# Where the weight splits stand around the last sums of a seven-product group, in a two-layer encoder trunk

## The chip, the core and the metric

The kernel runs on one core of one Trainium2 chip. The metric is the device time of one execution in microseconds; three runs of the kernel before gave 930.63, 929.8 and 930.38, so its median is 930.38 us.

The engines that matter here are TensorE (PE in the profile, with its weight loads as PEld), VectorE (DVE), ScalarE (ACT), GpSimd (POOL), which here mostly issues transfers that add to their destination, and SyncE (SP), which issues the plain transfers. Each engine works through its own instructions strictly in the order in which they were written into the program; an instruction waits until the data and the buffers that it needs are there, and everything behind it on the same engine waits with it.

## What is computed

The input is one sequence of 256 tokens of width 1024 in float32. There are two layers, each with a half-weighted SwiGLU channel mixer, a mixing part with two kinds of attention, and a second channel mixer; a norm closes the trunk. The channel mixers do most of the work:

```python
D_MODEL = 1024
SEQ = 256
DEPTH = 2
D_FF = 2816

def swiglu(h, w_gate, w_up, w_down):
    return (jax.nn.silu(h @ w_gate) * (h @ w_up)) @ w_down

    for l in range(DEPTH):
        x = x + 0.5 * swiglu(rms_norm(x, ffn1_norm[l]), ffn1_w_gate[l], ffn1_w_up[l], ffn1_w_down[l])
        ...
        x = x + jnp.concatenate([out_a, out_b], axis=-1) @ w_out[l]

        x = x + 0.5 * swiglu(rms_norm(x, ffn2_norm[l]), ffn2_w_gate[l], ffn2_w_up[l], ffn2_w_down[l])
    return rms_norm(x, final_norm)
```

## The kernel before

**Precision and the split.** Every float32 matrix is held as a sum of two parts in the type that TensorE multiplies fast: a high part, which is the value rounded by a cast on ACT, and a low part, which is the value less the high part, subtracted on DVE. A product is then three matmuls (high by high, low by high, high by low). So each weight tile that TensorE multiplies by must first be cast by ACT and subtracted by DVE. This pair of instructions is called a *split* here. The weights come in *steps* of 128 rows x 4 x 512 columns (1 MB), and each step is split in two halves, a and b, by `emit_split` (L191): `act.copy(h_, r_)` and `dve.tensor_tensor(l_, r_, f(h_), op=ALU.subtract)`.

**Groups.** A channel mixer goes through the 2816 hidden columns in five groups of 512 and a last one of 256. A group computes gate and up for 256 tokens, then the hidden block (silu of gate, times up). The hidden block is turned by TensorE (`turn`, L681: transposes, then a cast on ACT and a subtraction on DVE for each of two banks), so that it can be multiplied by the down weights, one group later: while group g works on its gate and up products, the down products of group g - 1 are woven in.

**Groups by seven products.** For some groups gate and up are not computed by eight products of a quarter of the work each (two token halves x two halves of the width x gate and up) but by seven, after the manner of Strassen and Winograd (`by_seven`, L632). The sums of tokens that this takes are made once in a channel mixer. The sums of weights are made in each group: two by transfers of POOL that add the incoming weights onto a tile in place (`gather`, L126), two by DVE (`plus`, L131; two instructions each, `prep` of a step). What the products give is put together by DVE additions (`put`, L637). `SEVEN` (L31) says which groups are done so: groups 2, 3 and 4 in the first channel mixer of the first layer, and groups 1, 2, 3 and 4 in the other three. These three are called *runs of four* here.

A group by seven products uses nine steps of weights, one after the other. Groups 2 to 4 use them in the order p1, p7, p2, p3, down 0, p5, p6, p4, down 1; the first group of a run (the branch `else` of `by_seven`) in the order p1, p2, down 0, p3, p7, p5, p6, p4, down 1. Each product is 12 matmuls of 128x512, each down product 24. The turn of the last group's hidden block stands behind p7 in groups 2 to 4. The end of a group is this: after p6, u2 = p6 - m1 and u3 = m7 + u2; after p4, g1 = p4 - u3, whose silu ACT takes; then u3 and u2 less p5, u2 plus p3, and two multiplications (`up`, L612) that make the hidden block's two halves from u2 and g0 and from u3 and g1. These are eight DVE instructions; the *last sums* are those from g1 on, and m1 and m7 are copies of p1 and p7 by ACT, g0 the gate of the first tokens.

**What sets the order.** All of this is kept in program order, and splits are written into the program ahead of their use. `weights()` (L249) hands out the next step; before that it calls `ahead(n)` (L228), which writes all splits up to half number n that can be written, and with them the sums of weights (`prep`) and the transfers of later steps. n is two times the number of the step, plus `look[0]`, less the argument `less`. When the second half of a step is first used, `Split.part` (L182) calls `ahead` once more, for one half further; with `held` set that call is left out. So `look[0]` is how many halves the splits stand ahead of the products, and where in the text `weights()` and the second halves stand decides between which other DVE and ACT instructions the splits fall. In a run of four `look[0]` is 8, 7, 6 and 5 in groups 1 to 4 (L734). Weights land in six buffers (`N_RAW`); a buffer is loaded again when the last split of its step is done, and the transfers of SP are issued in order.

Of the kernel before, what the change touches and what calls it, by code (L numbers as in the profile page):

```python
# [34 lines left out]
def trunk(ctx: ExitStack, tc: tile.TileContext, x, n1, g1, u1, d1, nm, w_in, sink,  # L35
# [21 lines left out]
    pe, act, dve, pool = Kept(nc.tensor), Kept(nc.scalar), Kept(nc.vector), Kept(nc.gpsimd)  # L57
# [9 lines left out]
    def nm_(s):  # L67
        uid[0] += 1
        return f"{s}_{uid[0]}"

    def bank():
        return ps.tile([P, 512], F32, tag="ps", bufs=8, name=nm_("ps"))
# [4 lines left out]
    def blk(dt=F32R):  # L77
        return s4.tile([P, 2, 512], dt, tag="s4", name=nm_("s4"))

    def tmp(tag="tmp", bufs=5, shape=(P, 2, 256), dt=F32):  # L80
        return tp.tile(list(shape), dt, tag=tag, bufs=bufs, name=nm_(tag))
# [143 lines left out]
    look = [IN_MIX]  # L225
    at = dict(use=0, dma=2, prep=2, split=4)

    def ahead(n):  # L228

        n = min(n, 2 * len(specs) - 1)  # L230
        while True:
            if at["split"] <= n and at["prep"] > at["split"] // 2:
                for _ in emit_split(*divmod(at["split"], 2)):
                    pass
                at["split"] += 1
            elif at["prep"] <= min(n // 2 + 1, len(specs) - 1) and at["dma"] > at["prep"] and \
                    (specs[at["prep"]].prep is None or at["split"] >= 2 * at["prep"]):
                if specs[at["prep"]].prep is not None:
                    specs[at["prep"]].prep()
                at["prep"] += 1  # L240
            elif at["dma"] < min(at["use"] + AHEAD, len(specs)) and (specs[at["dma"]].moves is None or len(raws) < N_RAW):
                if specs[at["dma"]].moves is not None:
                    for _ in emit_dma(at["dma"]):
                        pass
                at["dma"] += 1
            else:
                break

    def weights(less=0, held=False):  # L249

        i = at["use"]
        at["use"] += 1
        if i > 1:
            ahead(2 * i + look[0] - less)
        w = loaded[i]
        w.held = held
        return w
# [179 lines left out]
    norm = Norm(0)  # L437
# [90 lines left out]
    def tokens(accs, xs, w, k0, ks=range(4), first=0, last=KC - 1, order=None, cols=slice(None), h=None):  # L528

        for k, t in (order or [(k, t) for k in ks for t in range(2)]):  # L530
            kk = k0 + k
            hi, lo = w.part(k, cols, h)
            xv = xs[kk // 2][:, kk % 2]
            xh, xl = xv[:, t * P:(t + 1) * P], xv[:, S + t * P:S + (t + 1) * P]
            pe.matmul(accs[t], lhsT=xh, rhs=hi, start=kk == first, stop=False)
            pe.matmul(accs[t], lhsT=xl, rhs=hi, start=False, stop=False)
            pe.matmul(accs[t], lhsT=xh, rhs=lo, start=False, stop=kk == (last if isinstance(last, int) else last[t]))
# [62 lines left out]
    def ffn(norm, aside=None, before=None, final=False, sevens=SEVEN[1]):  # L600
        def silu(out_, acc, t):
            act.activation(out_, acc, AF.Silu, scale=norm.r[:, t:t + 1])
            return out_

        def gate(gs):
            g = []
            for t in range(2):
                n = gs[t].shape[1]
                g.append(silu(tmp().rearrange("p a n -> p (a n)")[:, :n], gs[t], t))
            return g  # L610

        def up(h, acc, g, t):  # L612
            n = acc.shape[1]
            dve.scalar_tensor_tensor(h[:, t, :n], in0=acc, scalar=norm.hr[:, t:t + 1], in1=g, op0=ALU.mult, op1=ALU.mult)
# [7 lines left out]
        def prod(xo, w):  # L622
            acc = bank()
            for k in range(4):
                hi, lo = w.part(k)
                xh, xl = xo(k)
                pe.matmul(acc, lhsT=xh, rhs=hi, start=k == 0, stop=False)
                pe.matmul(acc, lhsT=xl, rhs=hi, start=False, stop=False)
                pe.matmul(acc, lhsT=xh, rhs=lo, start=False, stop=k == 3)
            return acc  # L630

        def by_seven(h, g):  # L632


            flat = lambda: tmp().rearrange("p a n -> p (a n)")

            def put(o, x, y, op):  # L637
                dve.tensor_tensor(o, x, y, op=op)
                return o

            m1, m7 = flat(), flat()
            if g > 1:
                act.copy(m1, prod(norm.quarter(0, 0), weights()))
                act.copy(m7, prod(norm.summed(3), weights(held=True)))
                hT = turn(h, 2)
                p2 = prod(norm.quarter(0, 1), weights())
                g0 = put(flat(), p2, m1, ALU.add)
                p3 = prod(norm.summed(2), weights())
                silu(g0, g0, 0)
                down(hT, g - 1, 0, weights())  # L650
            else:
                p1 = prod(norm.quarter(0, 0), weights(1, True))
                hT = turn(h, (0,))
                w = weights(1, True)
                act.copy(m1, p1)
                p2 = prod(norm.quarter(0, 1), w)
                hT += turn(h, (1,))
                g0 = put(flat(), p2, m1, ALU.add)
                silu(g0, g0, 0)
                down(hT, 0, 0, weights())  # L660
                p3 = prod(norm.summed(2), weights())
                act.copy(m7, prod(norm.summed(3), weights()))
            h = blk(F32)
            p5 = prod(norm.summed(0), weights())
            late = g == max(sevens)
            p6 = prod(norm.summed(1), weights(look[0] - 5 if late else 0, late))
            u2 = put(flat(), p6, m1, ALU.subtract)
            u3 = put(m7, m7, u2, ALU.add)
            p4 = prod(norm.quarter(1, 1), weights(look[0] - 4 if late else 0, late))
            g1 = put(m1, p4, u3, ALU.subtract)  # L670
            w = weights(look[0] - 3 if late else 0)
            silu(g1, g1, 1)
            put(u3, u3, p5, ALU.subtract)
            put(u2, u2, p5, ALU.subtract)
            put(u2, u2, p3, ALU.add)
            up(h, u2, g0, 0)
            up(h, u3, g1, 1)
            down(hT, g - 1, 1, w)
            return h

        def turn(hs, n):  # L681
            out_ = []
            for i in (range(n) if isinstance(n, int) else n):
                sl = halves(bank())
                for c in range(2):
                    for t in range(2):
                        pe.transpose(sl[:, c, t * P:(t + 1) * P], hs[:, t, (2 * i + c) * P:(2 * i + c + 1) * P], ident)
                hb = blk()
                split(hb, sl)
                out_.append(hb)  # L690
            return out_
# [3 lines left out]
        def down(hT, g, h, w):  # L695
            tokens(accs[h], [None] * (2 * g) + hT, w, 4 * g, last=(FC - 1, G4 - 1) if final and h else FC - 1)
# [17 lines left out]
        if 1 in sevens:  # L714
            sums = norm.make_sums()
            next(sums)
            w = weights()
# [3 lines left out]
            w = weights(0, True)  # L721
            g = gate(gs)
            next(sums)
        else:
            tokens(gs, norm.xs, weights(), 4)
            g = gate(gs)
            w = weights()
# [4 lines left out]
        for n in range(1, NGRP):  # L732
            if n in sevens:
                look[0] = IN_FFN + min(sevens) - n if before is not take_x else IN_MIX - (n == NGRP - 1)  # L734
                h = by_seven(h, n)
                continue
            sums = norm.make_sums()
            gs = [bank(), bank()]
            tokens(gs, norm.xs, weights(), 0)
            hT = turn(h, 2)  # L740
            norm.copies()
            next(sums, None)
            tokens(gs, norm.xs, weights(), 4)
            g = gate(gs)
            next(sums, None)
            us = [bank(), bank()]
            for k0 in (0, 4):
                tokens(us, norm.xs, weights(), k0)
                next(sums, None)
            h = hidden(g, us)  # L750
            for hh in range(2):
                down(hT, n - 1, hh, weights())
                if hh == 0:
                    next(sums, None)
# [3 lines left out]
        hT = turn(h, 2)  # L758
# [303 lines left out]
    for l in range(DEPTH):  # L1062
# [7 lines left out]
        if not final:  # L1070
            norm = Norm((l + 1) * 8)
# [76 lines left out]
```

## Time and profile before

| what | value |
|---|---|
| median of three runs | 930.38 us |
| the profiled execution, its own time | 931.78 us |
| span of its trace | 930.0 us |
| granted TensorE clock, mean | 0.999 |
| PE busy | 911.6 us |
| DVE busy | 806.7 us |
| ACT busy | 590.8 us |
| POOL busy | 64.8 us |
| the three runs of four, by the trace (first to last of them) | about 316 to 430, 496 to 609, 774 to 887 us |

Times in the trace count from the start of the span; 1.78 us of the execution's own time lie around the span. The profiled execution is 1.4 us over the median of the runs, so differences are worked out against its span and then set upon the median. A line of the timeline gives the start, the length, the engine, the operation with what it writes and reads, how many instructions are merged in it, and in brackets the time for which the engine had been idle before it and what ended that. `w<-raw` on ACT is a cast of weights, `w<-raw,w` on DVE the subtraction of the same half, `raw<-raw,raw` a sum of weights, `tmp<-...` the additions of the products, `s<-tmp,hr,tmp` the two multiplications that make the hidden block, and `s<-ps` (ACT) and `s<-ps,s` (DVE) the split of the turned block. `ps<-ident,s` on PE is the turn. Almost everything has the line L50, as one helper issues it; so tiles, and not lines, tell instructions apart.

### The profile page before, as it was taken

The numbers are of one execution on the slowest core, as the hardware profiler recorded it, in microseconds if no ns is written. First come the engines' busy times: TensorE is split into PE (matmuls) and PEld (weight loads), VectorE is DVE, ScalarE is ACT, GpSimd is POOL, SyncE is SP. The second block draws the span as 40 slices with busy tenths as digits, with TensorE's granted clock in tenths as the row PEclk, the third lists the DMA queues.
The fourth block names the chain that finished last, engine by engine and source line by source line (L and its number), as shares of the span: only waits on it lengthen the run. The fifth ranks groups of instructions, "written<-read, shape, count | busy, mean of one in ns | idle before, by whom it ended". The sixth has DMA issues, their size and how long they took to land.

```text
span 930.0 us, 12604 instructions
## 1 busy us (share of the span) xinstructions
PE 911.6 (98%) x4696; PEld 763.4 (82%) x4696; DVE 806.7 (87%) x1125; ACT 590.8 (64%) x917; POOL 64.8 (7%) x83
## 2 busy tenths in 40 slices
PE   7999999999999999999999999999999999999997
PEld 6888887899888878787888788878998888788876
DVE  6769999969875899999779999997698679999994
ACT  7845675567755776576485766665578485676661
POOL 0401000000000101000010010000001010010011
PEclk9999999999999999999999999999999999999999
DMA  9987897837346598897776998887462376998831
GB/s 336 356 225 203 244 277 260 240 103 220 129 137 176 140 296 230 245 270 271 261 172 163 293 269 229 246 286 227 118 228 92 135 172 173 289 266 230 250 137 46
DMA packets 114061, 200.87 MB, mean 216 GB/s; under 512 B 3662, under 2 KB 31376, under 8 KB 114000
## 3 DMA queue, kind: packets, MB, share of 16 engines
q1 hardware_dynamic: 96528, 166.74, 53.0%
q0 software_dynamic: 16096, 31.75, 19.0%
q10 hardware_dynamic: 1376, 1.57, 0.5%
q8 instruction: 37, 0.61, 0.3%
q14 instruction: 24, 0.20, 0.1%
HBM read 199.00 MB, written 1.05 MB: 215 GB/s over the span
## 4 chain that ended last, share of the span: by engine, by line
PE 58%; DVE 27%; DMA 7%; issue 5%; ACT 2%; POOLq 0%; ACTq 0%; DVEq 0%; POOL 0%
PE ps L50 58%; DVE w L50 16%; DMA raw<-in_ffn_w_up_dram 7%; DVE raw L50 4%; DVE tmp L50 4%; DVE s L50 2%; ACT w L50 2%; DMA xk<-in_x_dram 1%; ACT tmp L50 0%; DVE v L50 0%; DVE q L50 0%; ACT s L50 0%; DVE xk L50 0%; ACTq L50 0%; POOLq L1143 0%
## 5 line engine op out<-in xcount | busy, mean ns | idle before, releaser
L50 PE MATMUL ps<-w,s 128*128 128x512 f32 (+1 forms) x2574 | 601.7, 391 | 1.9 <-DVE w L50 1.9
L50 PEld LDWEIGHTS ps<-w,s 128*128 128x128 f32 x2574 | 477.4, 188 | 101.7 <-DVE w L50 3.7
L50 DVE TENSOR_TENSOR w<-raw,w 128x1024 fp32r<-128x1024 f32 (+1 forms) x458 | 483.3, 1100 | 39.6 <-ACT w L50 38.9
L50 ACT CAST w<-raw 128x1024 fp32r<-128x1024 f32 (+1 forms) x458 | 410.5, 952 | 130.3 <-DVE raw L50 88.7
L50 PE MATMUL ps<-w,q 128*128 128x512 f32 x540 | 127.3, 389 | 0.0
L50 PEld LDWEIGHTS ps<-w,q 128*128 128x128 f32 x540 | 101.3, 188 | 21.1
L50 PE MATMUL ps<-s,w 128*128 128x256 f32 x672 | 84.0, 285 | 0.0
L50 PEld LDWEIGHTS ps<-s,w 128*128 128x128 f32 x672 | 81.7, 191 | 1.1
L50 POOL DMA_DIRECT2D raw<-in_ffn_w_up_dram x30 | 38.9, 1295 | 483.4 <-DVE w L50 205.4
L50 DVE TENSOR_TENSOR raw<-raw,raw 128x1024 f32<-128x1024 f32 x60 | 70.6, 1217 | 0.0
L50 ACT ACTIVATE s<-ps,gcol 128x256 fp32r<-128x256 f32 (+1 forms) x80 | 31.7, 480 | 46.8 <-PE ps L50 45.1
L50 ACT ACTIVATE tmp<-tmp,r 128x512 f32<-128x512 f32 x30 | 21.7, 722 | 43.0 <-DVE tmp L50 43.0
L50 PE MATMUL ps<-ident,s 128*128 128x128 f32 x304 | 43.8, 277 | 5.0 <-DVE s L50 4.8
L50 PEld LDWEIGHTS ps<-ident,s 128*128 128x128 f32 x304 | 34.6, 140 | 15.9 <-DVE s L50 11.5
L50 PE MATMUL ps<-w,v 128*128 128x512 f32 x180 | 43.6, 391 | 0.0
L50 ACT CAST s<-ps 128x512 fp32r<-128x512 f32 x44 | 24.2, 589 | 28.0 <-PE ps L50 27.7
L50 PEld LDWEIGHTS ps<-w,v 128*128 128x128 f32 x180 | 33.6, 188 | 7.9 <-issue 1.1
L50 ACT ACTIVATE s<-s,negm 128x256 f32<-128x256 f32 x64 | 31.9, 501 | 6.6 <-DVE negm L50 6.4
L50 DVE TENSOR_TENSOR tmp<-ps,tmp 128x512 f32<-128x512 f32 x49 | 33.4, 682 | 1.6 <-PE ps L50 1.6
L50 DVE SCALAR_TENSOR_TENSOR s<-ps,gcol,s 128x256 fp32r<-128x256 f32 x48 | 20.3, 478 | 14.9 <-ACT s L50 14.8
L50 DVE TENSOR_TENSOR s<-ps,s 128x512 fp32r<-128x512 f32 x44 | 28.6, 682 | 4.1 <-ACT s L50 4.1
L50 DVE TENSOR_TENSOR tmp<-tmp,ps 128x512 f32<-128x512 f32 x45 | 29.4, 681 | 0.5
(106 smaller groups left out, 396.0 us busy)
## 6 DMA issues: line engine op xcount, KB each, us to landing
raw<-in_ffn_w_down_dram SPq DMA_DIRECT2D x44, 1024.0 KB, 8.2
raw<-in_ffn_w_gate_dram SPq DMA_DIRECT2D x39, 1024.0 KB, 5.7
raw<-in_ffn_w_up_dram SPq DMA_DIRECT2D x39, 1024.0 KB, 5.2
raw<-in_ffn_w_up_dram POOLq DMA_DIRECT2D x30, 1024.0 KB, 11.9
raw<-in_w_in_dram SPq DMA_DIRECT2D x14, 1024.0 KB, 5.5
raw<-in_ffn_w_gate_dram SPq DMA_DIRECT2D x8, 512.0 KB, 7.0
raw<-in_ffn_w_up_dram SPq DMA_DIRECT2D x8, 512.0 KB, 8.0
raw<-in_w_in_dram SPq DMA_DIRECT2D x8, 512.0 KB, 5.4
```

The source lines that it names most:

```text
L50: ins = issue(*a, **k)
```

## The change

`run` is true in the three channel mixers that begin with group 1 by seven products (the runs of four), `late` in the last group of each. In the runs of four, p1 and p2 of groups 2 to 4 are handed out with two halves less ahead and `held`; p7 with three less (it was held already); p4 of groups 1 to 3 with one half less, and held; and down 1 of groups 1 to 3 is handed out with three less and held. In the last group p6, p4 and down 1 keep the arguments that they had. In the first group of a run the step of down 0 is handed out ahead of the silu of g0 rather than behind it. The channel mixer with three groups by seven products keeps its order.

```diff
             m1, m7 = flat(), flat()
+            late, run = g == max(sevens), 1 in sevens
             if g > 1:
-                act.copy(m1, prod(norm.quarter(0, 0), weights()))
-                act.copy(m7, prod(norm.summed(3), weights(held=True)))
+                act.copy(m1, prod(norm.quarter(0, 0), weights(2 * run, run)))
+                act.copy(m7, prod(norm.summed(3), weights(3 * run, True)))
                 hT = turn(h, 2)
-                p2 = prod(norm.quarter(0, 1), weights())
+                p2 = prod(norm.quarter(0, 1), weights(2 * run, run))
                 g0 = put(flat(), p2, m1, ALU.add)
...
                 g0 = put(flat(), p2, m1, ALU.add)
+                w = weights()
                 silu(g0, g0, 0)
-                down(hT, 0, 0, weights())
+                down(hT, 0, 0, w)
...
             p5 = prod(norm.summed(0), weights())
-            late = g == max(sevens)
             p6 = prod(norm.summed(1), weights(look[0] - 5 if late else 0, late))
             u2 = put(flat(), p6, m1, ALU.subtract)
             u3 = put(m7, m7, u2, ALU.add)
-            p4 = prod(norm.quarter(1, 1), weights(look[0] - 4 if late else 0, late))
+            p4 = prod(norm.quarter(1, 1), weights(look[0] - 4 if late else run, late or run))
             g1 = put(m1, p4, u3, ALU.subtract)
-            w = weights(look[0] - 3 if late else 0)
+            w = weights(look[0] - 3 if late else 3 * run, run and not late)
             silu(g1, g1, 1)
             put(u3, u3, p5, ALU.subtract)
             put(u2, u2, p5, ALU.subtract)
             put(u2, u2, p3, ALU.add)
             up(h, u2, g0, 0)
             up(h, u3, g1, 1)
             down(hT, g - 1, 1, w)
```

Every engine has the same instructions in both programs; on PE, POOL and SP they also stand in the same order. On DVE and ACT the order differs inside the three runs of four alone, from g0's silu of group 1 to g0 of group 4.

## The prediction

> **What bounds the kernel now.** I read the page's busy times first, then the chain that ended last, then the windows of one run of four, then the timelines of its engines.
>
> ```profile
> span 930.0 us, 12604 instructions
> PE 911.6 (98%) x4696; PEld 763.4 (82%) x4696; DVE 806.7 (87%) x1125; ACT 590.8 (64%) x917; POOL 64.8 (7%) x83
> ```
>
> Over the whole span PE looks like the only bound. The chain in order of time says otherwise for the runs of four:
>
> ```profile
> 428.39 1.22 DVE w L50
> 429.66 60.21 PE ps L50 x278
> ...
> 607.79 1.22 DVE w L50
> 609.05 158.59 PE ps L50 x1002
> ...
> 885.55 1.22 DVE w L50
> 886.81 32.55 PE ps L50 x148
> ```
>
> Each run of four ends in the same way: PE takes over only when DVE has done one certain split, and from there PE alone is the chain for 60, 159 and 33 us. That split is the first half of p4 in the last group. So the time of the kernel hangs on when DVE finishes it, three times. The windows between a run's first and last group (stretch, length, then busy PE, PEld, DVE):
>
> ```profile
> 348.00:380.00 32.00, 31.48 (x141) 25.56 (x141) 31.36 (x33) 20.23 (x25) 2.57 (x2) 1.00 0.88 249
> 380.00:411.00 31.00, 30.68 (x139) 25.55 (x140) 30.90 (x33) 19.99 (x23) 2.57 (x2) 1.00 0.89 257
> ```
>
> DVE is busy for 31.36 of 32 and 30.90 of 31 us, as densely as PE. It has no room: what it loses inside a run it does not get back before the run's end. PE's timeline there:
>
> ```profile
> 344.13 2.96 PE L50 MATMUL ps<-w,v 128*128 128x512 f32 x12
> 347.87 0.33 PE L50 MATMUL ps<-ident,s 128*128 128x128 f32 x1 [0.78 <-DVE s L50]
> 348.54 0.98 PE L50 MATMUL ps<-ident,s 128*128 128x128 f32 x7 [0.34 <-DVE s L50]
> ...
> 379.66 0.33 PE L50 MATMUL ps<-ident,s 128*128 128x128 f32 x1 [0.18 <-DVE s L50]
> ...
> 429.66 2.56 PE L50 MATMUL ps<-w,s 128*128 128x512 f32 x10 [0.46 <-DVE w L50]
> ```
>
> The turn waits for the hidden block (0.78 + 0.34, then 0.18 us), and at 429.66 PE waits again, for the split. A wait removed at 347.87 alone comes back at 429.66, since DVE's finish there does not depend on it.
>
> **The measure of the change.** In both programs the same DVE instructions stand ahead of that split, in another order. So per run the change in time is the change in DVE's idle time ahead of it, plus what the new neighbours cost each other. I keep this account for the run of 316 to 430 us. DVE's rows before:
>
> ```profile
> 318.85 0.68 DVE L50 TENSOR_TENSOR tmp<-ps,tmp 128x512 f32<-128x512 f32 x1
> 321.32 2.36 DVE L50 TENSOR_TENSOR w<-raw,w 128x1024 fp32r<-128x1024 f32 x2 [1.79 <-ACT w L50]
> ...
> 339.70 0.68 DVE L50 TENSOR_TENSOR tmp<-ps,tmp 128x512 f32<-128x512 f32 x1
> 340.42 0.69 DVE L50 TENSOR_TENSOR tmp<-tmp,tmp 128x512 f32<-128x512 f32 x1
> 341.03 2.35 DVE L50 TENSOR_TENSOR w<-raw,w 128x1024 fp32r<-128x1024 f32 x2
> ...
> 348.40 3.49 DVE L50 TENSOR_TENSOR w<-raw,w 128x1024 fp32r<-128x1024 f32 x3
> 351.80 1.28 DVE L50 TENSOR_TENSOR s<-ps,s 128x512 fp32r<-128x512 f32 x2
> ...
> 364.38 5.77 DVE L50 TENSOR_TENSOR w<-raw,w 128x1024 fp32r<-128x1024 f32 x5 [0.33 <-ACT w L50]
> 370.35 1.23 DVE L50 TENSOR_TENSOR w<-raw,w 128x1024 fp32r<-128x1024 f32 x1 [0.20 <-ACT w L50]
> ...
> 380.18 1.22 DVE L50 TENSOR_TENSOR w<-raw,w 128x1024 fp32r<-128x1024 f32 x1
> ...
> 411.25 3.49 DVE L50 TENSOR_TENSOR w<-raw,w 128x1024 fp32r<-128x1024 f32 x3
> ```
>
> A split takes 1.22 us and the next starts 1.13 us after it (348.40 to 351.80, three of them: 3.40). ACT's and the transfers' rows:
>
> ```profile
> 316.96 0.59 ACT L50 CAST s<-ps 128x512 fp32r<-128x512 f32 x1 [0.22 <-PE ps L50]
> 319.62 0.72 ACT L50 ACTIVATE tmp<-tmp,r 128x512 f32<-128x512 f32 x1 [2.08 <-DVE tmp L50]
> 320.25 1.98 ACT L50 CAST w<-raw 128x1024 fp32r<-128x1024 f32 x2
> ...
> 346.53 0.58 ACT L50 COPY tmp<-ps 128x512 f32<-128x512 f32 x1
> ...
> 361.73 1.05 ACT L50 CAST w<-raw 128x1024 fp32r<-128x1024 f32 x1 [3.02 <-DVE raw L50]
> 362.69 0.72 ACT L50 ACTIVATE tmp<-tmp,r 128x512 f32<-128x512 f32 x1
> ...
> 369.26 1.06 ACT L50 CAST w<-raw 128x1024 fp32r<-128x1024 f32 x1 [1.12 <-DMA raw<-in_ffn_w_up_dram]
> ```
>
> **1. Down 0's step ahead of the silu (group 1).** Before, the silu of g0 at 319.62 waits 2.08 us for g0 (DVE, 318.85), and the two casts of p5 stand behind it; DVE idles 1.79 us for them. In the changed order both casts and p6's first stand ahead of the silu. ACT is free for them at 316.96 + 0.59 = 317.55, the first ends near 318.6, before DVE is done with g0 near 319.45: the 1.79 us go. The silu now falls between the casts of p6's two halves. At 362.69 the same thing stands between two casts already, and DVE's next split idles 0.33 us (364.38): I take that. g0 is read first by the multiplication at the group's end, some 20 us later, so the later silu costs nothing else. Term: -1.79 + 0.33 = **-1.46 us**.
>
> **2. The sums stand next to each other (groups 1 to 3).** An addition that reads what the one before it wrote starts 0.72 us after it (339.70 to 340.42), one followed by an unrelated split 0.61 (340.42 to 341.03). With the splits gone from between them, u3 to g1 and g1 to the next sum become neighbours that depend: 2 x 0.12 = 0.24 us a group, **+0.72 us** a run. The Trainium skill (VectorE: DVE Perf Modes, "The DRAIN you can't avoid") says that the next operation starts only when the pipeline is empty, with or without a semaphore between; by it this term would be 0 and the whole sum 2.2 us smaller. The rows differ: the split at 341.03 starts before the addition ends at 341.11, so the rows decide.
>
> **3. The turn after group 1.** Before, three halves (two at 341.03, one between the sums) stand ahead of the hidden block and three behind it, until the turned block's subtraction at 351.80. Now the first three stand behind the block, and then at once that subtraction. The block is ready at 348.40 - 1.46 + 0.24 - 3 x 1.13 = 343.8, some 4.6 us earlier, and PE's wait of 0.78 + 0.34 is gone. But the turn is written behind p7, which ends on PE at 344.13 + 2.96 = 347.1; then ACT copies p7 (0.58, row 346.53) and casts the turned block (0.59): 348.3. DVE has 343.8 + 3.4 = 347.2 us of work. It idles **1.1 us**, on the engine that has none to spare. Behind the two casts ACT takes 1.05 for the next weights, until about 349.9, while DVE's two subtractions (1.28) end at 349.5: another **0.35**. After this DVE stands at -1.46 + 0.24 + 1.45 = +0.23 us against before.
>
> **4. p7's transfer in group 3.** Its cast at 369.26 waited 1.12 us for an adding transfer; DVE idled 0.20.
>
> ```profile
> 351.92 0.37 SPq L153 DMA_DIRECT2D raw<-in_ffn_w_up_dram  x1
> ...
> 357.58 1.29 POOL L50 DMA_DIRECT2D raw<-in_ffn_w_up_dram  x1 [18.50 <-DMA raw<-in_ffn_w_up_dram]
> ```
>
> The chain is: last split of down 0 (done 351.9) frees the buffer, SP loads (351.92), POOL adds (357.58), ACT casts (369.26). Now that split stands behind both subtractions of the turn, 2 x 0.60 later, and DVE is 0.23 late: +1.4 for the chain. DVE comes to the same place only 0.23 later, so its idle time grows from 0.20 to about 1.4: **+1.2 us**. SP and POOL keep their orders; what is queued behind this load on SP (issued from 357.65 on by the trace) is released by DVE itself later. If the transfers go faster with less beside them this is 0; if both legs (5.7 us to 357.58, 11.7 us to 369.26) are 10% slower it is 2.9. I take 1.2. DVE: +1.4.
>
> **5. The turn after group 2.** Here p7's second half itself is among the three halves moved behind the block. The block is ready at 380.18 + 1.4 + 0.24 - 3.4 = 378.4, the split is done at 379.6, and PE still has four matmuls (0.23 each, 2.96 / 12 with the start) of p7: about 380.7. Copy and cast: 381.9. DVE is through its three halves at 381.8: 0.1, and 0.3 behind the casts as in 3: **+0.4**. DVE: +2.1.
>
> **6. The turn after group 3.** `look[0]` has shrunk again and now both halves of p7 stand behind the block: ready at 411.25 + 2.1 + 0.24 - 3.4 = 410.2, first half split at 411.3, and ten matmuls remain: 413.8. Copy and cast: 415.0. DVE is through at 413.6: 1.4, and 0.3 behind the casts: **+1.7**. DVE: **+4.0 us** at the last group's p4. PE cannot undercut this: its turn is at 413.8 instead of
>
> ```profile
> 411.10 1.28 PE L50 MATMUL ps<-ident,s 128*128 128x128 f32 x8
> ```
>
> and it meets late halves of p2 behind it; the four waits that went (1.6 us) are less than those that came.
>
> The sum by run: -1.46 + 0.72 + 1.45 + 1.2 + 0.4 + 1.7 = 4.0. The other two runs have the same order of instructions, and the first term's idle time is there as well:
>
> ```profile
> 500.89 1.23 DVE L50 TENSOR_TENSOR w<-raw,w 128x1024 fp32r<-128x1024 f32 x1 [1.79 <-ACT w L50]
> ...
> 778.68 2.36 DVE L50 TENSOR_TENSOR w<-raw,w 128x1024 fp32r<-128x1024 f32 x2 [1.79 <-ACT w L50]
> ```
>
> Three times 4.0 is 12.0 us: span 930.0 to 942.0, the profiled execution 931.78 to 943.8 and the median 930.38 to **942.4 us**, 1.3% slower.
>
> **The rivals.** *PE is the bound, DVE's splits have slack enough.* Then the change is worth the waits at the turns, 0.78 + 0.34 + 0.18 and the 0.34 that recurs there, 1.6 us a run, 4.9 us in all: 925.5. For it speaks that PE is busy 98%; against it the wait at 429.66 and the two windows. The Trainium skill (Perfetto Trace Analysis, "Identifying the Most-Contended Engine") takes the engine of highest occupancy as the one to free, though it warns of just this number for matmuls; by it this rival would be the forecast. Chance 5%. *The turns do not starve DVE* (the copies come sooner than I count, or ACT catches up): terms 1, 2 and 4 stay, +0.5 a run, 931.8, no change that can be told. Against it: p7's end at 347.1 is PE's own pace. Chance 5%. *The lateness feeds on itself*: buffers come free later in every group, and the adding transfers of group 4 become late as p7's is in group 3, twice 1.2 us more a run, 7 us in all: 949.6. For it: casts already wait for these transfers (369.26); against: in group 4 they are needed later than DVE is held up anyway. Chance 10%. *The change does not do what it says* is out: in the built order no split stands between u2 and the second multiplication in groups 1 to 3.
>
> **How the numbers follow.** My forecast, slower by some 6 to 15 us, has 80%, the rivals 5, 5 and 10. Below, the sum without term 4 and with half of the turns' idle time (1.8) is 1.0 a run, 933.4; above, with term 4 at 2.9, 5.7 a run, 947.5. As terms fail seldom together, the range is 936 to 947. About 0.2% (1.9 us) is what a measurement of this kernel can tell from none: faster 5%, same 5%, slower 90%.
>
> **What would show it.** Right: DVE's 1.79 us of idle time in group 1 gone; new idle time of over 1 us on DVE ahead of the turned block's subtraction after groups 1 and 3, and ahead of p7's first half in group 3; PE's turns no longer waiting for the hidden block but p7 for DVE's splits; each run about 4 us longer, the first channel mixer unchanged. Wrong: DVE without idle time through the runs, or runs that end no later than now.

## The result and the profile after

The changed kernel took 946.11 us (median of 6 runs, 943.9 to 947.44), the kernel before 930.32 (6 runs, 929.8 to 930.63): a ratio of 1.0168, 95% interval 1.0154 to 1.0182. The forecast was 942.4 with a range of 936 to 947. The page of the changed kernel's profiled execution, first the span and the busy times, then the group of p7's matmuls (count, then busy time and mean ns of one, then the idle time ahead of them):

```profile
span 945.7 us, 12580 instructions
PE 914.7 (97%) x4696; PEld 761.6 (81%) x4696; DVE 810.1 (86%) x1125; ACT 589.1 (62%) x917; POOL 65.2 (7%) x83
...
L50 PE MATMUL ps<-w,v 128*128 128x512 f32 x180 | 45.1, 394 | 7.7 <-DVE w L50 7.7
```

The span is 15.7 us longer, but PE is busy for only 3.1 us more and DVE for 3.4, so most of the loss is idle time. Before, the matmuls of p7 (those that read `v`, the sums of tokens) had no idle time ahead of them; now 7.7 us, all for splits. The view of waits (total us, times, longest) of the changed kernel:

```profile
PEld ps L50 <- DVE w L50: 21.9, 22, 1.7
...
PE ps L50 <- DVE w L50: 13.2, 17, 1.3
```

The same rows before:

```profile
PEld ps L50 <- DVE w L50: 3.7, 4, 1.0
PE ps L50 <- DVE w L50: 1.9, 4, 0.5
```

PE waits for DVE's splits 17 times instead of 4, and its weight loads 22 times instead of 4. The chain that ended last shows where the runs of four end now (start, us, what):

```profile
434.07 1.22 DVE w L50
435.33 60.21 PE ps L50 x278
...
619.51 158.54 PE ps L50 x1002
...
901.21 1.22 DVE w L50
902.48 32.55 PE ps L50 x148
```

These are the rows of 428.39, 607.79 and 885.55 before: the same split, then the same 60, 159 and 33 us of PE. It comes 5.68 us later at the end of the first run and 15.66 at the end of the third. DVE's timeline in the first run of the changed kernel:

```profile
321.11 2.34 DVE L50 TENSOR_TENSOR w<-raw,w 128x1024 fp32r<-128x1024 f32 x2
...
327.28 1.23 DVE L50 TENSOR_TENSOR w<-raw,w 128x1024 fp32r<-128x1024 f32 x1 [0.34 <-ACT w L50]
...
340.05 2.36 DVE L50 TENSOR_TENSOR w<-raw,w 128x1024 fp32r<-128x1024 f32 x2 [2.33 <-ACT w L50]
342.32 0.68 DVE L50 TENSOR_TENSOR tmp<-ps,tmp 128x512 f32<-128x512 f32 x1
343.04 0.69 DVE L50 TENSOR_TENSOR tmp<-tmp,tmp 128x512 f32<-128x512 f32 x1
343.84 0.69 DVE L50 TENSOR_TENSOR tmp<-ps,tmp 128x512 f32<-128x512 f32 x1
344.56 2.01 DVE L50 TENSOR_TENSOR tmp<-tmp,ps 128x512 f32<-128x512 f32 x3
...
351.35 1.28 DVE L50 TENSOR_TENSOR s<-ps,s 128x512 fp32r<-128x512 f32 x2
...
411.71 3.48 DVE L50 TENSOR_TENSOR w<-raw,w 128x1024 fp32r<-128x1024 f32 x3
416.69 1.29 DVE L50 TENSOR_TENSOR s<-ps,s 128x512 fp32r<-128x512 f32 x2 [1.49 <-ACT s L50]
```

The 1.79 us ahead of p5's splits (321.32 before, 321.11 now) are gone. But at 340.05, ahead of p7's first half in group 2, 2.33 us of idle time stand that no step of the prediction has. The turn after group 1 (351.35) has none; the turn after group 3 (416.69) has 1.49, as forecast. PE there, in the changed kernel:

```profile
411.05 0.61 PE L50 MATMUL ps<-w,v 128*128 128x512 f32 x2
412.98 2.56 PE L50 MATMUL ps<-w,v 128*128 128x512 f32 x10 [1.31 <-DVE w L50]
415.38 1.03 PE L50 MATMUL ps<-ident,s 128*128 128x128 f32 x8
```

p7 has done 2 of its 12 matmuls and waits 1.31 us for the split of its first half; the turn then follows without a wait, at 415.38 instead of 411.10.

To divide the loss I took the start of the same split in both traces, after less before, and from one place to the next what had been added:

| DVE's loss, us | forecast, a run | run 1 | run 2 | run 3 | sum |
|---|---|---|---|---|---|
| p5 to p4, group 1 (term 1) | -1.46 | -1.45 | -1.44 | -1.44 | -4.33 |
| p7 of group 2 (no term) | 0 | +2.40 | +0.58 | +0.62 | +3.60 |
| sums and turn after group 1 (2, 3) | +1.69 | +0.34 | +0.74 | +0.70 | +1.78 |
| p7 of group 3 (term 4) | +1.2 | -0.27 | +1.89 | +2.37 | +3.99 |
| sums and turn after group 2 (2, 5) | +0.64 | +0.85 | +0.84 | +0.85 | +2.54 |
| sums and turn after group 3 (2, 6) | +1.94 | +2.15 | +2.17 | +2.16 | +6.48 |
| a run | +4.0 | +4.02 | +4.78 | +5.26 | +14.06 |

The runs lost 14.06 us of the 15.7 in the spans. The other 1.66 were there before the first run began, in the first channel mixer, whose instructions stand in the same order in both programs. From the chains of waits, an adding transfer there, first in the changed kernel, then in the one before:

```profile
79.44 14.35 DMA raw<-in_ffn_w_up_dram
```

```profile
79.98 12.13 DMA raw<-in_ffn_w_up_dram
```

It took 14.35 us instead of 12.13. That is the scatter of one execution and not the change: at the first run's beginning the profiled executions of the experiments below stand between 1.58 us ahead of the one of before and 0.54 behind it. So losses are read from the runs of four, and whole kernels are compared by medians. By the medians the loss is 15.8 us; where the 1.7 us between that and the 14.06 come from, in executions without a trace, is open (the six of the changed kernel spread over 3.5 us).

### The profile page after: what moved, and what is told of

Its sections match the earlier page's. It is cut to its first block, busy times and chain, and to the rows that moved or that the text cites. A ratio compares the mean times of both kernels' runs of the same rounds, so it can differ in the third digit from the quotient of the medians.

```text
span 945.7 us, 12580 instructions
## 1 busy us (share of the span) xinstructions
PE 914.7 (97%) x4696; PEld 761.6 (81%) x4696; DVE 810.1 (86%) x1125; ACT 589.1 (62%) x917; POOL 65.2 (7%) x83
## 3 DMA queue, kind: packets, MB, share of 16 engines
HBM read 199.00 MB, written 1.05 MB: 212 GB/s over the span
## 4 chain that ended last, share of the span: by engine, by line
PE 66%; DVE 19%; DMA 6%; issue 4%; ACT 4%; POOLq 0%; ACTq 0%; POOL 0%; DVEq 0%
PE ps L50 66%; DVE w L50 11%; DMA raw<-in_ffn_w_up_dram 6%; DVE tmp L50 4%; DVE raw L50 3%; ACT w L50 2%; DVE s L50 1%; ACT s L50 1%; ACT tmp L50 1%; DMA xk<-in_x_dram 1%; DVE xk L50 0%; ACTq L50 0%; POOLq L1145 0%; POOL rf L50 0%; DVEq L50 0%
## 5 line engine op out<-in xcount | busy, mean ns | idle before, releaser
L50 PE MATMUL ps<-w,s 128*128 128x512 f32 (+1 forms) x2574 | 606.0, 392 | 10.4 <-DVE w L50 5.6
L50 PE MATMUL ps<-ident,s 128*128 128x128 f32 x304 | 41.7, 275 | 1.8 <-DVE s L50 1.7
L50 ACT COPY tmp<-ps 128x512 f32<-128x512 f32 x34 | 19.8, 582 | 21.9 <-PE ps L50 21.9
```

The source lines that it names most:

```text
L50: ins = issue(*a, **k)
```

## The experiments

Each expectation states its own theories. Ratios are to the kernel before on the same chip, whose medians there were 930.78 (23 runs; the silu's edit alone, the sums' edits alone and the two kernels at the end of group 3), 931.49 (11 runs; the three with a late load and the end of group 1) and 930.85 (9 runs; the end of group 2).

**The silu's edit alone.** Kernel before, with only this:

```diff
+                w = weights()
                 silu(g0, g0, 0)
-                down(hT, 0, 0, weights())
+                down(hT, 0, 0, w)
```

> Only down 0's step is handed out ahead of g0's silu in group 1 of each run of four; all else as before. Theory A (my account): DVE's 1.79 us of idle time go and 0.33 come, nothing starves because the splits around the last sums stay, so each run is about 1.5 us shorter: near 926 us. Rival B (what DVE gains early it gives back at a transfer): the plain load behind the sums of weights is issued some 1.8 us sooner, runs beside the adding transfer for p7 of group 2, that one takes some 2.3 us longer (13.3 instead of 10.8 in the changed kernel), and DVE idles for it: 0 to 1 us a run longer, 930 to 933 us.

929.73 us, ratio 0.9986 (0.9976 to 0.9996): theory A's 926 did not come, and rival B's range of 930 to 933 was missed by 0.3 us. The 1.46 us were gained in each run, and 2.46, 0.9 and 0.54 us were given back at p7 of group 2, as rival B had it, so that the first run became 0.8 us longer, the others 0.5 and 1.0 shorter. The chain of waits of this kernel in its first run shows what took it:

```profile
317.71 5.10 DMA raw<-in_ffn_w_up_dram
323.37 13.24 DMA raw<-in_ffn_w_up_dram
336.69 1.06 ACT w L50
```

The adding transfer of p7 lands 13.24 us after its issue, ACT casts, and DVE, idle for 2.37 us, starts p7's splits only at 337.77:

```profile
337.77 2.36 DVE L50 TENSOR_TENSOR w<-raw,w 128x1024 fp32r<-128x1024 f32 x2 [2.37 <-ACT w L50]
```

What made it so long can be read from the transfers beside it. The transfer queues of SP and POOL in the kernel before:

```profile
325.98 0.37 SPq L153 DMA_DIRECT2D raw<-in_ffn_w_gate_dram  x1
...
323.91 1.28 POOL L50 DMA_DIRECT2D raw<-in_ffn_w_up_dram  x1 [19.29 <-DVE w L50]
```

and with the silu's edit alone:

```profile
323.45 0.37 SPq L153 DMA_DIRECT2D raw<-in_ffn_w_gate_dram  x1
...
323.37 1.28 POOL L50 DMA_DIRECT2D raw<-in_ffn_w_up_dram  x1 [19.39 <-DMA raw<-in_ffn_w_up_dram]
```

This profiled execution came to the run 0.65 us earlier, and the adding transfer starts 0.54 us earlier, so at its old place. But the next plain load on SP, that of 325.98, now comes at 323.45. It waits for a buffer that the sum of weights for p6 (`raw<-raw,raw` on DVE) reads last; that sum follows p5's splits, so with the 1.79 us of idle time gone it ends that much earlier too. The two transfers of 1 MB used to start 2.07 us apart and now start within 0.1 us of each other. Their times to landing before:

```profile
raw<-in_ffn_w_up_dram POOLq DMA_DIRECT2D x1, 1024.0 KB, 10.8
...
raw<-in_ffn_w_gate_dram SPq DMA_DIRECT2D x1, 1024.0 KB, 9.9
```

and with the silu's edit alone:

```profile
raw<-in_ffn_w_up_dram POOLq DMA_DIRECT2D x1, 1024.0 KB, 13.2
raw<-in_ffn_w_gate_dram SPq DMA_DIRECT2D x1, 1024.0 KB, 5.8
```

The load, which nobody needs soon, takes 5.8 instead of 9.9 us; the adding transfer, which the next split needs, 13.2 instead of 10.8.

**The sums' edits alone.** The changed kernel with the silu where it was:

```diff
-                w = weights()
                 silu(g0, g0, 0)
-                down(hT, 0, 0, w)
+                down(hT, 0, 0, weights())
```

> The changed kernel without the edit at g0's silu: splits kept out of the last sums in groups 1 to 3, the silu as before. Theory A: the turn after group 1 no longer starves DVE, since DVE is later there, but the turns after groups 2 and 3 and p7's transfer in group 3 cost as they did: 4 to 5 us a run, 943 to 946 us, no better than the changed kernel. Rival B (the transfers beside each other make most of the loss): without the earlier load at least 2 us a run are saved, 937 to 940 us.

944.89 us, ratio 1.0146 (1.0131 to 1.0161), as theory A had it. The runs lost 3.69, 4.89 and 5.28 us. That is as much as in the changed kernel itself, so there the silu's gain is wholly lost. Term 3 is not seen here either (+0.33): DVE still has its 1.79 us of idle time and comes to the turn as late as p7 does.

**The silu's edit, with the load kept late.** The first experiment, and behind p6's casts in group 1 a copy on ACT of one column of the buffer in question into an unused tile, which only makes the buffer free later:

```diff
             act.copy(h_, r_)
             dve.tensor_tensor(l_, r_, f(h_), op=ALU.subtract)
...
+            if s.linger is not None:
+                act.copy(scrap, raws[s.linger][:, 0, 0:1])
```

> The kernel with the edit at g0's silu alone, and with a copy of one column by ACT that reads the buffer to be loaded next, written behind the casts of p6 in group 1 (the column is used nowhere). So the plain load that started 0.1 to 0.2 us behind the adding transfer for p7 of group 2 starts about 1.7 us later, as in the kernel before. Theory B (the two transfers beside each other give the 1.46 us back): the adding transfer takes 10.8, 9.2 and 9.2 us again as before, DVE's 1.46 us a run are kept: 930.8 - 4.4 = 926.4 us. Rival E (DVE, early by then, waits for the same data anyway, or PE sets the end): the adding transfer is short but the run's end does not move, 929.5 to 930.5 us.

926.65 us, ratio 0.9954 (0.994 to 0.9967): 4.8 us less than before, where the edit without the copy was worth 1. The queues of SP and POOL of this kernel, and then its adding transfer's time to landing:

```profile
324.32 0.37 SPq L155 DMA_DIRECT2D raw<-in_ffn_w_gate_dram  x1
...
322.60 1.28 POOL L50 DMA_DIRECT2D raw<-in_ffn_w_up_dram  x1 [19.35 <-DMA raw<-in_ffn_w_up_dram]
```

```profile
raw<-in_ffn_w_up_dram POOLq DMA_DIRECT2D x1, 1024.0 KB, 10.4
```

1.72 us apart, and 10.4 instead of 13.2 us. No idle time is left ahead of p7's split in group 2, and the time is theory B's. The next load on SP kept its distance from the adding transfer (327.77 - 322.60 = 5.17 us, 328.49 - 323.37 = 5.12 without the copy), so the held load alone has moved. This shows the cause: the load's start beside the adding transfer.

**The changed kernel with the load kept late.** The same copy in the changed kernel.

> The changed kernel with the same later load. Theory A: DVE then comes 1.5 us early to the turn after group 1 and starves there for about 1 us, as the forecast had it; what p7's transfer gives back the turn takes: 943 to 946 us, not clearly faster than the changed kernel, with idle time of DVE ahead of the turned block's subtraction instead of ahead of p7's first half. Rival B (the collision is a cost of its own): 0.5 to 2.4 us a run less than the changed kernel, 940 to 943 us.

944.49 us, ratio 1.0148 (1.0129 to 1.0167). p7 of group 2 costs nothing now, and yet the kernel is hardly faster than the changed one. DVE's timeline at the turn after group 1 says why:

```profile
342.58 3.49 DVE L50 TENSOR_TENSOR w<-raw,w 128x1024 fp32r<-128x1024 f32 x3
346.76 1.29 DVE L50 TENSOR_TENSOR s<-ps,s 128x512 fp32r<-128x512 f32 x2 [0.69 <-ACT s L50]
348.19 3.50 DVE L50 TENSOR_TENSOR w<-raw,w 128x1024 fp32r<-128x1024 f32 x3
```

A punctual DVE waits 0.69 us for the turned block, and the splits behind its two subtractions start 1.43 us after the first of them (348.19 - 346.76), where 2 x 0.60 would do: term 3, which neither of the other kernels had in this size. With the dependent sums this place costs 1.34 to 1.36 us in the three runs. So of the 3.6 us that p7 of group 2 no longer costs, this place takes 2.3 and p7 of group 3, now at 1.0, 1.5 and 2.1 us, another 0.7.

**The edit at the end of group 1 alone** (the arguments of group 1's p4 and down 1, and of group 2's p1, p7 and p2; the silu as before):

```diff
+            late, on = g == max(sevens), 1 in sevens
+            run = on and g == 1
+            nxt = on and g == 2
...
-                act.copy(m7, prod(norm.summed(3), weights(held=True)))
+                act.copy(m7, prod(norm.summed(3), weights(3 * nxt, True)))
...
-            w = weights(look[0] - 3 if late else 0)
+            w = weights(look[0] - 3 if late else 3 * run, run and not late)
```

> The edit at the end of group 1 and the beginning of group 2 alone. Theory A: 0.3 us a run for the sums next to each other, no starving at the turn since DVE is not early, but p7's transfer in group 3 comes late, because the load ahead of it waits for down 0's last split, which now stands behind the turn's subtractions: 0.3 to 1.9 us of idle time there, as in the run with the sums alone; 932 to 937 us. Rival C (only the sums): 931.5 us.

936.61 us in one run, 5.1 above the median of before, in a profiled execution that came to the first run 1.58 us early. The runs lost 1.72, 2.08 and 2.69 us. 0.33 of each are the dependent sums, 1.39, 1.75 and 1.67 stand ahead of p7's first half in group 3, and the third run lost 0.7 more ahead of p7 of group 4. DVE's rows of this kernel:

```profile
347.13 1.28 DVE L50 TENSOR_TENSOR s<-ps,s 128x512 fp32r<-128x512 f32 x2
...
370.48 1.23 DVE L50 TENSOR_TENSOR w<-raw,w 128x1024 fp32r<-128x1024 f32 x1 [1.59 <-ACT w L50]
```

The turn (347.13) has no wait, but 1.59 us of idle time stand at p7 where 0.20 stood (370.35). So term 4 comes from this edit alone, which lets down 0's last split stand behind the turn and with it the load that follows that split.

**The edit at the end of group 2 alone** (the same with groups 2 and 3).

> The edit at the end of group 2 and the beginning of group 3 alone, with the silu as before. Theory A (the turn after group 2 costs its own small sum, whatever DVE's lateness): dependent sums 0.31 a run, p7's second half behind the hidden block and the wait for the copy and the cast of the turned block 0.5 to 0.7 a run, as the run of all the sums showed +0.87 at this place; p7 of group 3 is split as before, so its adding transfer costs nothing: 0.8 to 1.1 a run, 2.4 to 3.3 us over the kernel before, about 934. Theory B (the 0.87 was a consequence of the lateness that p7's transfer in group 3 had brought): with DVE punctual only the dependent sums stay, 0.3 a run, 1 us in all. Theory C (a punctual DVE waits longer at the turn, since PE reaches it no sooner): 1.5 a run or more, 4.5 us and up.

934.47 us, ratio 1.0041 (1.0024 to 1.0059). The runs lost 0.79, 0.91 and 0.99 us, as theory A had it. DVE's row at the turn has the short wait of term 5 and no other:

```profile
380.85 1.29 DVE L50 TENSOR_TENSOR s<-ps,s 128x512 fp32r<-128x512 f32 x2 [0.19 <-ACT s L50]
```

**The edit at the end of group 3 alone** (the same with groups 3 and 4).

> The edit at the end of group 3 and the beginning of group 4 alone, in each run of four. Theory A: both halves of p7 stand behind the hidden block, DVE starves at the turn for about 1.5 us and the sums next to each other cost 0.3: 2 us a run, near 936.5 us. Rival C (only the dependent sums next to each other cost something): 0.3 us a run, near 931.3 us.

938.75 us, ratio 1.0071 (1.0057 to 1.0086). The runs lost 2.06, 2.21 and 2.24 us, all of it at the turn after group 3: theory A, though the median is over 2 us above its 936.5. DVE's rows there:

```profile
408.61 3.49 DVE L50 TENSOR_TENSOR w<-raw,w 128x1024 fp32r<-128x1024 f32 x3
413.60 1.29 DVE L50 TENSOR_TENSOR s<-ps,s 128x512 fp32r<-128x512 f32 x2 [1.50 <-ACT s L50]
```

**The same end of group 3, with p7 split ahead of the sums.** If term 6 comes from p7's halves standing behind the hidden block, it must go when they stand ahead of all the sums, with no split between the sums either:

```diff
-            p6 = prod(norm.summed(1), weights(look[0] - 5 if late else 0, late))
+            p6 = prod(norm.summed(1), weights(look[0] - 5 if late else (look[0] - 9) * run, late or run))
...
-            p4 = prod(norm.quarter(1, 1), weights(look[0] - 4 if late else 0, late))
+            p4 = prod(norm.quarter(1, 1), weights(look[0] - 4 if late else 9 * run, late or run))
...
-            w = weights(look[0] - 3 if late else 0)
+            w = weights(look[0] - 3 if late else 9 * run, run and not late)
```

(`run` in group 3 of the runs of four only)

> As the run before, with no split between the last sums of group 3, but with both halves of p7 written ahead of the sums and four halves between the hidden block and the turn. Theory A: no starving, 0.3 us a run for the sums: 931.3 us. Rival D (any delay of splits behind the block costs, wherever p7 stands): as with the run before, near 936.5 us.

933.72 us, ratio 1.0033 (1.002 to 1.0045), between the times of the two theories. DVE's rows:

```profile
402.07 2.36 DVE L50 TENSOR_TENSOR w<-raw,w 128x1024 fp32r<-128x1024 f32 x2 [0.49 <-ACT w L50]
...
414.50 1.28 DVE L50 TENSOR_TENSOR s<-ps,s 128x512 fp32r<-128x512 f32 x2
```

The 1.50 us at the turn are gone. What stays, 0.8 to 0.9 a run, is the dependent sums and 0.49 at 402.07, where p7 is now asked for a little before its adding transfer has landed. So a group's last sums without splits between them cost little; what was dear is where the displaced splits went.

**A version that beats both.** The silu's edit with the late load, and more of the same kind: in group 1 down 0's step is handed out one half further ahead, so that both of p6's casts stand ahead of the silu, and in groups 2 and 4 down 0's step stands ahead of the silu too. The sums are as before:

```diff
+                w = weights() if 1 in sevens and g != 3 else None
                 silu(g0, g0, 0)
-                down(hT, g - 1, 0, weights())
+                down(hT, g - 1, 0, weights() if w is None else w)
...
-                w = weights()
+                w = weights(-1)
                 silu(g0, g0, 0)
```

> As the run before, and the silu of g0 behind both casts instead of between two, in groups 1, 2 and 4 of each run of four. By DVE's account its idle times of 0.33 in group 1 (new), 0.33 in group 2 and 0.34 in group 4 go as well: 1.0 us a run more, 923.5 us if theory B holds for the run before and PE's own waits do not take over; at most the 3.1 us of PE's waits of a run can be had, so no less than 921 us. Rival E: 929 to 930 us.

925.12 us, ratio 0.9934 (0.9922 to 0.9945): 6.4 us under the kernel before on its chip, but 1.6 above the 923.5 that was expected. By DVE's account the runs are 1.2, 2.1 and 1.9 us shorter than before, where 2.5 each were counted: the idle time in group 2 only moved to another split (0.34 at 362.80), and in the first run 0.45 and 0.59 us were lost ahead of p7 of groups 2 and 3.

## Why the prediction was right, and where it was off

*The bound* was right. Each run became longer by 4.0 to 5.3 us, its end moved with DVE's split of p4, PE's 60, 159 and 33 us behind it did not change, and the waits of PE for the hidden block that the change removed bought nothing. "PE is the bound" fell with the sign, and "the turns do not starve DVE" with the 1.49 us at 416.69. The prediction has the first of these as the forecast by the Trainium skill (Perfetto Trace Analysis, "Identifying the Most-Contended Engine"); but that section judges TensorE by its weight loads and by its useful share of the peak, not by the matmuls' busy time. By the weight loads, 82% against DVE's 87%, it names DVE, as the runs do. The three edits at the turns alone lost 4.57, 5.20 and 5.92 us a run between them, the whole of them at once 3.69, 4.89 and 5.28: nearly a sum, with a little cover for one another.

*Term 1* was right at its place (-1.45 for -1.46, with the forecast 0.33 as 0.34 at 327.28). What failed is its last sentence, that the later silu "costs nothing else": I asked who reads g0, and not what a DVE that is 1.5 to 1.9 us earlier sets free. (Its "some 20 us" to the reader of g0 are 27 in the rows, 319.62 to 347.06; nothing hangs on it.) It frees a buffer, a load starts beside p7's adding transfer, and p7 of group 2 comes late: 3.60 us in three runs. The late-load experiment shows this cause.

*Term 2* was a little too small. The neighbours u3 and g1 start 0.80 us apart (343.04, 343.84) and not 0.72, so a group loses 0.80 - 0.61 + 0.72 - 0.60 = 0.31 us where 0.24 was forecast. The Trainium skill (VectorE: DVE Perf Modes, "The DRAIN you can't avoid") would have put it at nothing by its sentence that the next operation waits for the empty pipeline, with or without a semaphore. The same section adds that a next operation that is not held starts earlier, and the split at 341.03, ahead of the addition's end at 341.11, agrees with that.

*Term 3* was right as a mechanism and not there in this kernel: +0.34 to +0.74 with the sums instead of 1.69. It supposes a DVE that has kept the gain of term 1, and it had been held up at p7 11 us earlier (340.05, the turn at 351.35). The two are alternatives: DVE waits at whichever it reaches too soon. With the collision away, term 3 stood there with 1.05 (1.36 less the 0.31 of the sums), where 1.45 was forecast. (The row at 346.53 that the prediction reads as p7's copy is p1's; p7's, at 347.95, is as long.)

*Term 4* was 1.2 a run by a chain at its old speed. Its beginning was right: the load of the chain starts at 356.05 instead of 351.92, 4.13 us later, when DVE is 2.95 late, so 1.2 us late by itself. But neither leg kept its time: the load's took 6.7 us (356.05 to 362.78) instead of 5.7, and the adding leg did not keep its 11.7. In the second run the chain that ended last goes through it:

```profile
537.00 1.23 DVE w L50
...
538.25 4.89 DMA raw<-in_ffn_w_up_dram
...
543.70 12.31 DMA raw<-in_ffn_w_up_dram
```

The adding transfer took 9.1 us in the first run (term: -0.27), 12.31 in the second (+1.89) and 12.84 in the third (+2.37), on average 1.33 us a run for 1.2. That the mean comes so near is luck, with runs between -0.27 and +2.37.

*Terms 5 and 6* were right in place and cause, and each 0.2 us short: 0.85 for 0.64 and 2.16 for 1.94. 0.07 of it is term 2's; part of the rest is that an instruction that had to wait no longer overlaps the end of the one before it (408.61 + 3.49 = 412.10 is the end, and the next would have started at 412.01).

*The sum.* The step that was off is thus term 4's constant leg and term 1's silence on transfers together, +3.60 and +0.39, against term 3's 3.3 us that did not come; terms 5 and 6 with their sums add 1.3: 14.06 for 12.0. That two errors of about 3.5 us nearly cancelled is luck, as they were opposite sides of one thing. By its time alone 946.11 lies as near to the rival *the lateness feeds on itself* (949.6) as to the forecast (942.4); the places decide. That rival puts its cost at adding transfers of group 4, where the changed kernel has none; the longer transfers stand in groups 2 and 3. (In the experiments it shows once: 0.7 us at p7 of group 4, in the third run of the edit at the end of group 1 alone.)

## What to carry to other kernels

When an edit makes the bounding engine earlier, ask which buffers it then frees, which loads start on them, and beside which transfer that the engine needs next they will run: an edit that took 1.46 us of idle time away was worth a third of a microsecond a run until the freed load was held back by 1.7 us. Waits in series on one engine are alternatives and not terms of a sum: cost the later ones with the lateness that the earlier ones leave. And work that is moved out of a chain has to go where its own reader does not yet wait for it: the same bare sums cost 2.2 us a run with p7's splits behind them and 0.9 with them ahead.

## What the runs showed of the hardware

*Two transfers that start together are not served alike: one moves first, the other waits.* The plain load of 1 MB and the adding transfer of 1 MB, by the offset between their issues (load after add):

| place | load after add, us | adding transfer, us | load, us |
|---|---|---|---|
| p7, group 2, before | +2.07 | 10.8 | 9.9 |
| p7, group 2, late load | +1.72 | 10.4 | 9.9 |
| p7, group 2, after | +0.21 | 13.3 | 5.6 |
| p7, group 2, silu alone | +0.08 | 13.2 | 5.8 |
| p7, group 3, before | +0.07 | 11.6 | 5.7 |
| p7, group 3, after, run 2 | -0.32 | 12.3 | 5.5 |
| p7, group 3, after, run 1 | -1.59 | 9.1 | 5.0 |

Other loads follow on SP some 3 to 5 us later in all of them. A load that starts with the adding transfer lands nearly as fast as one well ahead of it (5.5 to 5.8 us against 5.0), and the adding transfer pays for it: at p7 of group 2 it took 13.2, 11.6 and 11.4 us in the three runs with the silu's edit alone, and 10.8, 9.2 and 9.2 before. With 2 us of lead the adding transfer lands sooner and the load takes 9.9.

The packets show how. In the view of transfers q0 is POOL's queue and q1 SP's; the rows give packets, MB and a share of the transfer engines' time. First the kernel before from 326.0 to 329.8 us, when both transfers had been issued; then the silu's edit alone from 323.5 to 327.7, likewise; last the same kernel from 332.5 to 333.5, still in this adding transfer but beside later loads:

```profile
q0 software_dynamic: 329, 0.67, 105.9%
...
q1 hardware_dynamic: 395, 0.81, 70.8%
...
q0 software_dynamic: 65, 0.13, 71.5%
q1 hardware_dynamic: 63, 0.13, 38.6%
```

In the first two stretches one queue has all packets and the other none. With 2 us of lead the adding transfer goes first and the load waits; issued together, the load goes first, and no packet of the adding transfer moves until 4.3 us after its issue (323.37 to 327.7). In the last stretch the two queues move equal numbers. The Trainium skill (DMA: Bandwidth & Descriptors, "Queues, rings and completion order") has each transfer engine go round its queues and move a whole packet of several descriptors from one before it turns to the next. The equal numbers agree with such turns. The first two stretches show no turns; how large such packets are here no run tells, and why the transfer that begins first is moved first is left open.

*The distance between two additions that depend on each other* was 0.72 us at most places and 0.80 from u3 to g1; a cause was not tried.
